# Hybrid decoder layer in float32: two plain weight loads moved ahead of the quarter B22 on SyncE's queue

## The chip, the cores and the metric

One core of one Trainium2 chip. The metric is device time in microseconds of one execution, as the median of three runs. Inputs and outputs are float32 in HBM; the weights (about 277 MB) are read once, in pieces of 512 KB.

## What is computed

One decoder layer for 256 tokens, D_MODEL 2048, D_FF 5632, 16 heads of 128. Cut to what matters:

```python
h = rmsnorm(x, g_mix)
proj = h @ w_in                                 # 2048 x (3*2048 + 3*2048): q, k, v and three gates
gates = sigmoid(proj[..., 3 * MIX_WIDTH:])
...                                             # three attention branches on q, k, v
merged = (gates[:, :, 0] * (flat(o_a) @ w_branch[:ea])
          + gates[:, :, 1] * (flat(o_b) @ w_branch[ea:eb])
          + gates[:, :, 2] * (flat(o_c) @ w_branch[eb:]))
x = x + merged @ w_out
h2 = rmsnorm(x, g_ffn)
gu = h2 @ w_gu                                  # 2048 x (2*5632)
x = x + (silu(gu[..., :D_FF]) * gu[..., D_FF:]) @ w_down
```

## The kernel before, in words

**Numbers in two halves.** Every float32 operand is split into a high part, rounded to the type that TensorE multiplies at full rate, and a low part, the rest. `split` (L108) does it with a cast on ScalarE (`w_hi`) and a subtraction on VectorE (`w_lo`). `product` (L161) then makes one product of three matmuls, hi*hi (L163), hi*lo (L164) and lo*hi (L165); each has 128 rows of weights and streams 512 columns into one PSUM bank.

**Stages.** First q, k, v and the gates (`w_in`), with attention work fed in between; then the branch projections (`w_branch`), the output projection (`w_out`), the FFN's first product (`w_gu`) and its second (`w_down`).

**Pairs.** q with k (4 times), two gate columns (5 times) and the FFN's gate and up columns (11 times) are computed by `project_pair` (L324): two columns of 512, A and B, against the 256 tokens at once. Of the 2048 rows of the weights, the first 1024 (two chunks of 512, `WC`) go through a scheme of seven products in place of eight: the weights of a chunk are four quarters B11, B12, B21 and B22 (first or second half of its rows, column A or B), and the seven forms multiply sums of the quarters with sums of the activations that are kept ready. The other 1024 rows are plain: four loads per column, which the prediction calls k0 to k3 for column B. One pair holds 180 matmuls of 512 columns.

The four PSUM banks of a pair are X, Y, Z and V (named `ps`/`qs` and, from the second gates pair on, `z`/`v` in the profile). The order of the program is: form 1 (B11) into X, snapshot of X; form 2 (B21) into Y; form 5 (u, the sum of B11 and B12) into Z, snapshot of Z; then the loads of B22; then plain k0 and k1 into V and Z; u += B22 and form 6 (u) into X, snapshot; plain k2; B12 += B22 and form 7 into X, snapshot; plain k3; form 3 (B22) into Z; and then column A: plain k0, k1, u += B21, form 4, plain k2, k3. A snapshot (L304) is a copy by ScalarE; the bank goes on being added to, so TensorE cannot write it again before the copy has read it. At its end a pair calls `begin_pair` (L314) for the next: this loads B11, B12 and B21 and splits B11 and B21.

**Loads.** `load` (L281) issues one DMA of 512 KB on SyncE's queue. Quarters go into `g_raw`, six buffers, two for each quarter (one per chunk); plain loads go into `w_raw`, four buffers. With six buffers for eight quarter loads per pair, the loads of B22 take the buffers of B11 of the same pair, and the plain loads k0 and k1 take the buffers of k0 and k1 of column A of the pair before. `fetch` (L104) pins these DMAs in the order of the program, and an instruction that waits on SyncE's queue holds all behind it. `parts` (L287) makes `w_hi` and `w_lo` of a load; there are five buffers of each, and every call also moves other work on by a step (`stages`).

**Order elsewhere.** The kernel runs under a scheduler that places the instructions of TensorE, VectorE and ScalarE by its own estimate of when their inputs are ready; only pinned ones keep the program's order. After a pair its results are taken over in the next one: for gates by `keep_gate` (L668), four sigmoid activations (L671) on ScalarE whose results GpSimd's queue writes out (L672); for the FFN two activations (L861) and two products (L862).

Of the kernel before, what the change touches and what calls it, by code (L numbers as in the profile page):

```python
# [56 lines left out]
def hybrid_block(ctx: ExitStack, tc: tile.TileContext, x, w_in, w_branch, w_out, w_gu, w_down, rel_bias, xT, gains,  # L57
# [24 lines left out]
    def pool(stack, name, side, bufs=1):  # L82
        return stack.enter_context(tc.tile_pool(name=name, bufs=bufs, side=side, reuse_waits="tile"))
# [8 lines left out]
    def half_kb(dt=F32):  # L92

        return scratch.tile([P, NB], dt, name="sc")
# [3 lines left out]
    def banks():  # L98

        turn.reverse()  # L100
        return [acc.tile([P, NB], F32, name=turn[1]) for _ in range(2)]
# [6 lines left out]
    def split(hi, lo, src, pin=False):  # L108
        for op in nc.scalar.copy(hi, src), nc.vector.tensor_sub(lo, src, hi.bitcast(F32)):  # L109
            if pin:  # L110
                tc.keep_in_program_order(op)
# [19 lines left out]
    def advance(queue):  # L131
        while queue:
            try:
                next(queue[0])
                return
            except StopIteration:
                queue.pop(0)
# [23 lines left out]
    def product(ps, ah, al, wh, wl, start=False, stop=False):  # L161
        how = dict(skip_group_check=True)
        nc.tensor.matmul(ps, ah, wh, start=start, stop=False, **how)  # L163
        nc.tensor.matmul(ps, ah, wl, start=False, stop=False, **how)  # L164
        nc.tensor.matmul(ps, al, wh, start=False, stop=stop, **how)  # L165
# [115 lines left out]
    def load(w, k, col0, pl=None):  # L281

        raw = pl.tile([P, 2, NB], F32, name="g_raw", bufs=6 if pl is gx else 4) if pl else wpool.tile([P, 2, NB], F32, name="w_raw", bufs=4)
        (nc.sync.dma_start if w is w_down else fetch)(raw, w[k * P:(k + 2) * P, col0:col0 + NB].rearrange("(k p) n -> p k n", p=P))
        return raw

    def parts(src):  # L287
        hi = wpool.tile([P, 2, NB], F32R, name="w_hi")
        lo = wpool.tile([P, 2, NB], F32R, name="w_lo")
        split(hi, lo, src)  # L290
        advance(stages)
        split_count[0] += 1
        if split_count[0] % 2:
            advance(slow_stages)
        for step in at_split.pop(split_count[0], ()):
            step()
        return hi, lo
# [4 lines left out]
    def snapshot(ps):  # L302
        sb = half_kb()
        nc.scalar.copy(sb, ps)  # L304
        return sb

    def add_into(dsts, srcs):
        for d, a in zip(dsts, srcs):
            tc.keep_in_program_order(nc.vector.tensor_add(d, d, a))  # L309

    def quarter(acts, w, kh, col0):
        return [load(w, 4 * c + 2 * kh, col0, gx) for c in acts.wc]

    def begin_pair(acts, w, colA, colB):  # L314

        b11, b12 = (quarter(acts, w, 0, col0) for col0 in (colA, colB))
        p11 = [parts(b) for b in b11]
        u = [gx.tile([P, 2, NB], F32, name="u") for _ in acts.wc]
        for a, b, d in zip(b11, b12, u):
            nc.vector.tensor_add(d, a, b)  # L320
        b21 = quarter(acts, w, 1, colA)
        return p11, b12, u, b21, [parts(b) for b in b21]

    def project_pair(acts, w, colA, colB, begun=None, nxt=None):  # L324

        cols = (colA, colB)
        X, Y = banks()
        Z, V = others()  # L330

        def form(ps, f, srcs, start, stop, split=False):
            for i, c in enumerate(acts.wc):
                wh, wl = srcs[i] if split else parts(srcs[i])
                for j in range(2):
                    product(ps, *acts.form(f, c, j), wh[:, j], wl[:, j], start and i + j == 0,
                            stop and i + j == len(acts.wc))

        def rest(n, k, p0, p1, start=False, stop=False):
            wh, wl = parts(load(w, k, cols[n]))  # L340
            for t, ps in ((1, p1), (0, p0)):
                for j in range(2):
                    product(ps, *acts.plain(t, k + j), wh[:, j], wl[:, j], bool(start and t == 1 and j == 0), stop and j == 1)

        ks = [k for c in range(KT // 4) if c not in acts.wc for k in (4 * c, 4 * c + 2)]
        p11, b12, u, b21, p21 = begun or begin_pair(acts, w, colA, colB)
        form(X, 1, p11, True, True, True)
        s1 = snapshot(X)
        form(Y, 2, p21, True, False, True)
        form(Z, 5, u, True, True)  # L350
        z5 = snapshot(Z)
        b22 = quarter(acts, w, 1, colB)
        rest(1, ks[0], Z, V, start=True)
        rest(1, ks[1], Z, V)
        add_into(u, b22)
        form(X, 6, u, False, True)
        x2 = snapshot(X)
        rest(1, ks[2], Z, V)
        add_into(b12, b22)
        form(X, 7, b12, False, True)  # L360
        x3 = snapshot(X)
        rest(1, ks[3], Z, V, stop=True)
        nc.vector.tensor_sub(z5, z5, x3)
        c22 = half_kb()
        nc.vector.tensor_add(c22, V, z5)
        form(Z, 3, b22, False, True)
        c12 = half_kb()
        nc.vector.tensor_sub(c12, Z, x2)
        for k in ks[:2]:
            rest(0, k, Y, X)  # L370
        add_into(u, b21)
        form(X, 4, u, False, False)
        for k in ks[2:]:
            rest(0, k, Y, X, stop=k == ks[-1])
        ahead = begin_pair(*nxt) if nxt else None
        c11 = half_kb()
        nc.vector.tensor_add(c11, Y, s1)
        return (c11, X, c12, c22), ahead
# [9 lines left out]
    p1 = pool(ph1, "p1", "left")  # L388
# [343 lines left out]
    for (kind, what), after in zip(units, units[1:] + [(None, None)]):  # L732
        if kind == "gates" and what[0] == chunks[4]:
            finish_stages(slow_stages)
            pat.close()
            acc2 = ctx.enter_context(tc.tile_pool(name="acc2", bufs=1, space=PSUM))
            others = beside
            o = Columns(pool(ph1, "o", "left"), "o", NH)
            for i in range(NH // 4):
                at_split[split_count[0] + 22 * i + 14] = [lambda k=4 * i: split_o(k)]  # L740
        nxt = pair_of(*after)
        if kind in ("qk", "gates"):
            ps, ahead = project_pair(*pair_of(kind, what), ahead, nxt)
            if others is in_turn:
                turn.reverse()
        else:
            ps = project(h, 0, w_in, 0, KT, V0 + what * NB if kind == "v" else gate_col(*what),
                         *((ps0, FIRST) if (kind, what) == ("v", 0) else ()))
            ahead = begin_pair(*nxt) if nxt else None
        finish_stages(stages)  # L750
        if kind == "v":
            keep_v(what, ps)
        elif kind == "qk":
            keep_qk(what, *ps)
        elif kind == "gate":
            keep_gate(*what, ps)
        else:
            keep_gate(*what[0], ps[:2])
            keep_gate(*what[1], ps[2:])
# [96 lines left out]
    for c in range(D_FF // NB):  # L856
        nxt = (h2, w_gu, (c + 1) * NB, D_FF + (c + 1) * NB) if c + 1 < D_FF // NB else None
        (g0, g1_, u0, u1), ahead = project_pair(h2, w_gu, c * NB, D_FF + c * NB, ahead, nxt)
        sg = [half_kb() for _ in range(NT)]
        for t, (g, u) in enumerate(((g0, u0), (g1_, u1))):  # L860
            nc.scalar.activation(sg[t], g, AF.Silu, scale=rstd2[:, t:t + 1])  # L861
            nc.vector.scalar_tensor_tensor(sg[t], u, rstd2[:, t:t + 1], sg[t], op0=ALU.mult, op1=ALU.mult)  # L862
        stages.append(to_a(c, sg))
# [153 lines left out]
```

## Time and profile before

| what | value |
| --- | --- |
| median of 3 runs | 1430.11 us (1429.63 to 1432.79) |
| the profiled execution, its own time | 1431.52 us |
| its span, first to last instruction | 1429.8 us |
| granted TensorE clock, mean | 1.00 |
| busy: TensorE, VectorE, ScalarE, GpSimd | 99%, 83%, 62%, 5% |
| HBM read, mean rate | 293.17 MB, 215 GB/s over the span |
| the last three gates pairs (w_in) | about 424 to 545 us |
| FFN pairs (w_gu) | about 730 to 1190 us |

In rows of single instructions the first number is the start in us from the span's start, the second the duration in us, then engine, line, operation, and output <- inputs by the program's names. PE is TensorE, ACT ScalarE, DVE VectorE, SPq SyncE's queue; a number in brackets is the idle time of the engine ahead of the instruction and what ended it. Rows that begin with one engine's name and an arrow say for whom it waited, in us: in total, how often, the longest. Rows that begin with a stretch (A:B) give its length, then TensorE's busy time and instructions in it, the granted clock, and the DMA share and rate. The end of a matmul is modelled, so starts are more reliable than ends.

### The profile page before, as it was taken

To read this page: it belongs to the slowest core of one execution; us is meant where nothing else is said; L and a number is where in the kernel's file an instruction comes from. 1 tells how busy PE (TensorE), PEld (TensorE's weight loads), DVE (VectorE), ACT (ScalarE), POOL (GpSimd) and SP (SyncE) were. 2 spreads that over 40 slices of the span, in tenths; PEclk is the share of its full clock that TensorE was granted. 3 is DMA by queue.
4 is the path that set the end of the run, shared out by engine and by line. 5 is a ranking of instruction groups with operands and counts; after the bars stand their busy time and mean duration, and the time that the engine had idled before them with its cause. 6 is when DMAs were issued, how large, how long until landed. Compare 5 with 4: busy or idle time off the path is not lost.

```text
span 1429.8 us, 17687 instructions
## 1 busy us (share of the span) xinstructions
PE 1416.7 (99%) x6369; PEld 1167.6 (82%) x6369; DVE 1192.8 (83%) x1265; ACT 881.4 (62%) x1136; POOL 65.2 (5%) x121
## 2 busy tenths in 40 slices
PE   9999999999999999999999999999999999999998
PEld 6888788888887778888888888888888888788887
DVE  7898797857798886876689999999999998886775
ACT  7777777667666665444457666666666666554453
POOL 1000000000000002100100000000000010100000
PEclk9999999999999999999999999999999999999999
DMA  9864547374656757876786556666665666767552
GB/s 327 279 221 134 206 137 245 112 247 157 222 188 223 254 195 268 297 229 213 222 299 221 198 182 218 224 226 227 220 210 192 231 212 230 251 235 235 190 172 95
DMA packets 155048, 309.05 MB, mean 216 GB/s; under 512 B 10792, under 2 KB 13376, under 8 KB 154960
## 3 DMA queue, kind: packets, MB, share of 16 engines
q1 hardware_dynamic: 144672, 277.38, 57.7%
q0 software_dynamic: 8992, 29.45, 6.1%
q10 hardware_dynamic: 1296, 1.08, 0.2%
q8 instruction: 50, 0.82, 0.2%
q14 instruction: 38, 0.31, 0.1%
HBM read 293.17 MB, written 14.70 MB: 215 GB/s over the span
## 4 chain that ended last, share of the span: by engine, by line
PE 81%; DVE 8%; DMA 4%; issue 3%; ACT 2%; SPq 0%; DVEq 0%; ACTq 0%
PE ps L164 9%; PE qs L164 9%; PE qs L165 9%; PE ps L165 9%; PE ps L163 9%; PE qs L163 9%; DVE w_lo L109 4%; PE z L163 4%; PE z L164 4%; PE z L165 4%; PE v L164 2%; PE v L165 2%; PE v L163 2%; DMA w_raw<-in_w_in 2%; PE tr L185 1%
## 5 line engine op out<-in xcount | busy, mean ns | idle before, releaser
L109 DVE TENSOR_TENSOR w_lo<-w_raw,w_hi 128x1024 fp32r<-128x1024 f32 x332 | 403.1, 1221 | 110.9 <-ACT w_hi L109 107.5
L109 ACT CAST w_hi<-w_raw 128x1024 fp32r<-128x1024 f32 x332 | 346.4, 1051 | 167.4 <-PE qs L165 59.9
L109 ACT CAST w_hi<-g_raw 128x1024 fp32r<-128x1024 f32 x184 | 192.2, 1053 | 146.9 <-PE ps L165 42.9
L109 DVE TENSOR_TENSOR w_lo<-g_raw,w_hi 128x1024 fp32r<-128x1024 f32 x184 | 219.6, 1221 | 35.1 <-ACT w_hi L109 33.8
L109 ACT CAST w_hi<-u 128x1024 fp32r<-128x1024 f32 x138 | 144.9, 1053 | 141.4 <-DVE u L309 71.3
L109 DVE TENSOR_TENSOR w_lo<-u,w_hi 128x1024 fp32r<-128x1024 f32 x138 | 165.7, 1220 | 24.9 <-ACT w_hi L109 24.0
L164 PE MATMUL ps<-w_lo,h_hi 128*128 128x512 f32 x352 | 137.9, 392 | 1.5 <-DVE w_lo L109 1.5
L165 PE MATMUL ps<-w_hi,h_lo 128*128 128x512 f32 x352 | 137.3, 390 | 0.0
L163 PE MATMUL ps<-w_hi,h_hi 128*128 128x512 f32 x352 | 132.4, 391 | 0.0
L164 PE MATMUL qs<-w_lo,h_hi 128*128 128x512 f32 x332 | 129.7, 391 | 0.0
L165 PE MATMUL qs<-w_hi,h_lo 128*128 128x512 f32 x332 | 129.2, 390 | 0.0
L163 PE MATMUL qs<-w_hi,h_hi 128*128 128x512 f32 x332 | 123.6, 391 | 0.0
L309 DVE TENSOR_TENSOR u<-u,g_raw 128x1024 f32<-128x1024 f32 x80 | 94.6, 1218 | 0.0
L164 PEld LDWEIGHTS ps<-w_lo,h_hi 128*128 128x128 f32 x352 | 66.1, 188 | 15.9 <-DVE w_lo L109 2.3
L165 PEld LDWEIGHTS ps<-w_hi,h_lo 128*128 128x128 f32 x352 | 66.1, 188 | 13.6
L163 PEld LDWEIGHTS ps<-w_hi,h_hi 128*128 128x128 f32 x352 | 65.9, 188 | 13.4
L165 PEld LDWEIGHTS qs<-w_hi,h_lo 128*128 128x128 f32 x332 | 62.4, 188 | 12.9
L164 PEld LDWEIGHTS qs<-w_lo,h_hi 128*128 128x128 f32 x332 | 62.4, 188 | 12.7
L163 PEld LDWEIGHTS qs<-w_hi,h_hi 128*128 128x128 f32 x332 | 62.3, 188 | 12.7
L320 DVE TENSOR_TENSOR u<-g_raw 128x1024 f32<-128x1024 f32 x40 | 48.6, 1218 | 22.7 <-DMA g_raw<-in_w_in 18.4
L164 PE MATMUL v<-w_lo,h_hi 128*128 128x512 f32 x120 | 47.4, 395 | 1.8 <-DVE w_lo L109 1.8
L163 PE MATMUL v<-w_hi,h_hi 128*128 128x512 f32 x120 | 47.7, 397 | 0.1
(383 smaller groups left out, 2925.8 us busy)
## 6 DMA issues: line engine op xcount, KB each, us to landing
w_raw<-in_w_in SPq DMA_DIRECT2D x116, 512.0 KB, 4.8
g_raw<-in_w_gu SPq DMA_DIRECT2D x88, 512.0 KB, 5.1
w_raw<-in_w_gu SPq DMA_DIRECT2D x88, 512.0 KB, 6.2
g_raw<-in_w_in SPq DMA_DIRECT2D x72, 512.0 KB, 5.9
w_raw<-in_w_down SPq DMA_DIRECT2D x64, 512.0 KB, 4.6
w_raw<-in_w_branch SPq DMA_DIRECT2D x32, 512.0 KB, 5.9
w_raw<-in_w_out SPq DMA_DIRECT2D x32, 512.0 KB, 4.8
g_raw<-in_w_down SPq DMA_DIRECT2D x24, 512.0 KB, 5.1
```

The source lines that it names most:

```text
L109: for op in nc.scalar.copy(hi, src), nc.vector.tensor_sub(lo, src, hi.bitcast(F32)):
L163: nc.tensor.matmul(ps, ah, wh, start=start, stop=False, **how)
L164: nc.tensor.matmul(ps, ah, wl, start=False, stop=False, **how)
L165: nc.tensor.matmul(ps, al, wh, start=False, stop=stop, **how)
L185: nc.tensor.transpose(pt[:, i, :], src[:, i * P:(i + 1) * P], ident)
L309: tc.keep_in_program_order(nc.vector.tensor_add(d, d, a))
L320: nc.vector.tensor_add(d, a, b)
```

## The change

In `project_pair`, the plain loads k0 and k1 of column B are issued ahead of the two loads of B22 and handed to `rest`, which loads by itself only when it is given nothing:

```diff
-        def rest(n, k, p0, p1, start=False, stop=False):
-            wh, wl = parts(load(w, k, cols[n]))
+        def rest(n, k, p0, p1, start=False, stop=False, raw=None):
+            wh, wl = parts(raw or load(w, k, cols[n]))
...
         z5 = snapshot(Z)
+        first = [load(w, k, cols[1]) for k in ks[:2]]
         b22 = quarter(acts, w, 1, colB)
-        rest(1, ks[0], Z, V, start=True)
-        rest(1, ks[1], Z, V)
+        rest(1, ks[0], Z, V, start=True, raw=first[0])
+        rest(1, ks[1], Z, V, raw=first[1])
         add_into(u, b22)
```

So the order on SyncE's queue, per pair, goes from six quarter loads, two of B22, k0, k1, k2, k3 to six quarter loads, k0, k1, two of B22, k2, k3. The number of loads, their sizes and the buffers stay. The scheduler, which sees the new order, also places some instructions anew:

- TensorE: in the third to fifth gates pair and the second FFN pair the first matmul of k0 into V stands ahead of the last eleven of form 5 into Z, instead of behind them; in some of the first FFN pairs a few more matmuls and transposes change places.
- ScalarE: in the same four pairs the cast of k0 stands ahead of the activations that take over the pair before. In the first FFN pair one cast of form 7 goes ahead of the snapshot of X; in the fifth the snapshot of Z goes ahead of both casts of form 6, and an activation pair (L861) between the casts of form 5.
- VectorE: nothing moves in the qk and gates pairs; in the first, second, fourth and fifth FFN pairs a few subtractions and small products change places.
- GpSimd: nothing moves.

## The prediction, made before the changed kernel had run

> **What bounds the kernel now.** I read the page first, then the busy time by windows, then the single matmuls around each place where TensorE stops.
>
> ```profile
> span 1429.8 us, 17687 instructions
> PE 1416.7 (99%) x6369; PEld 1167.6 (82%) x6369; DVE 1192.8 (83%) x1265; ACT 881.4 (62%) x1136; POOL 65.2 (5%) x121
> ...
> 939.23:1190.00 250.77, 250.77 (x1131) 1.00 0.65 220
> ```
>
> TensorE is the bound: 99% of the span, and in the six FFN pairs from 939 to 1190 us it never stops. So the order of loads can only win back moments in which PE stood still. Busy time hides these in part, because each matmul's end is modelled. The starts show them:
>
> ```profile
> 466.97 0.39 PE L164 MATMUL qs<-w_lo,h_hi 128*128 128x512 f32 x1
> ...
> 469.24 0.39 PE L165 MATMUL qs<-w_hi,h_lo 128*128 128x512 f32 x1
> ...
> 474.45 0.39 PE L165 MATMUL z<-w_hi,b_slo 128*128 128x512 f32 x1
> 474.98 0.49 PE L163 MATMUL v<-w_hi,h_hi 128*128 128x512 f32 x1
> 476.24 0.50 PE L164 MATMUL v<-w_lo,h_hi 128*128 128x512 f32 x1 [0.77 <-DVE w_lo L109]
> 476.57 0.39 PE L165 MATMUL v<-w_hi,h_lo 128*128 128x512 f32 x1
> ```
>
> The first two are ten starts apart, so a 512-column matmul costs 2.27 / 10 = 0.227 us. From 474.45 to 476.57 three starts take 2.12 us in place of 0.68: this place cost 1.44 us. Two waits (0.53 - 0.227 and 1.26 - 0.227) make 1.33 of it; the 0.11 left over is a slow start after the wait (0.33 in place of 0.227). The matmuls that waited are the first of the plain load k0, into V. Who was late is read in the other engines:
>
> ```profile
> 447.82 8.50 SPq L106 DMA_DIRECT2D g_raw<-in_w_in  x6
> ...
> 465.09 1.50 SPq L106 DMA_DIRECT2D g_raw<-in_w_in  x2
> 466.65 17.04 SPq L106 DMA_DIRECT2D w_raw<-in_w_in  x7
> ...
> SPq L106 <- DVE w_lo L109: 25.2, 8, 8.7
> ...
> 466.65 7.15 DMA w_raw<-in_w_in
> ...
> 473.87 1.05 ACT L109 CAST w_hi<-w_raw 128x1024 fp32r<-128x1024 f32 x1 [1.62 <-DMA w_raw<-in_w_in]
> 475.18 1.05 ACT L109 CAST w_hi<-w_raw 128x1024 fp32r<-128x1024 f32 x1 [0.26 <-DMA w_raw<-in_w_in]
> ...
> 474.95 2.53 DVE L109 TENSOR_TENSOR w_lo<-w_raw,w_hi 128x1024 fp32r<-128x1024 f32 x2 [3.62 <-ACT w_hi L109]
> 477.40 2.35 DVE L309 TENSOR_TENSOR u<-u,g_raw 128x1024 f32<-128x1024 f32 x2
> ```
>
> SyncE issued b11, b12 and b21 by 456.32, then stood until 465.09: b22 needs the buffers of b11, and its queue's longest wait is 8.7 us, for the w_lo that reads them. Only then came k0, at 466.65, and it landed 7.15 us later. ScalarE sat idle 1.62 us for it, VectorE 3.62 us, and PE stopped. The chain is b22's buffer, k0's issue, k0's landing, cast, subtraction, matmul.
>
> **The change part by part.** It adds and removes no instruction and no byte. In each of the 20 pairs (4 qk, 5 gates, 11 FFN) two 512 KB loads pass the two of b22 on SyncE's queue; no other queue's order moves, GpSimd's included. What else moves is the scheduler's work, which I take from the built order.
>
> *The loads.* k0 and k1 now wait only for the w_raw buffers of the pair before:
>
> ```profile
> 451.30 1.22 DVE L109 TENSOR_TENSOR w_lo<-w_raw,w_hi 128x1024 fp32r<-128x1024 f32 x1
> ...
> DMA to landing us min/median/max: 3.5/6.1/12.3
> ...
> DMA to landing us min/median/max: 3.5/4.9/6.6
> ```
>
> The second of these is read out at 452.52, before b21's last issue ends at 456.32. So this wait is over when SyncE comes to it, and b22, which is queued behind it, is not held. k0 leaves at about 456.4. The first landing row is that of all w_raw loads from 400 to 560 us: 3.5 to 12.3 us puts k0 between 459.9 and 468.7, against 473.8. I take the median 6.1, 462.5. b22 still leaves at 465.09 and 466.22. By the second row (g_raw, same stretch) it lands by 472.8 at the latest; its first reader, the add at 477.40, will come at 475.8 (below). Both ends cost nothing, since the first cast of k0 cannot start before 469.67 anyway.
>
> *The casts, three gates pairs from 424 us on and the second FFN pair.* The built order puts k0's cast ahead of the L671 activations (L861 in the FFN).
>
> ```profile
> 467.17 2.19 ACT L109 CAST w_hi<-u 128x1024 fp32r<-128x1024 f32 x2 [1.89 <-PE ps L165]
> 471.69 0.56 ACT L304 COPY sc<-qs 128x512 f32<-128x512 f32 x1
> ...
> 476.13 0.58 ACT L304 COPY sc<-z 128x512 f32<-128x512 f32 x1
> ```
>
> w_hi has five buffers, so k0's cast needs the matmuls of b11's second half, whose last starts at 469.24 and ends 0.39 later, and 0.03 from one engine to the next (the cast ends at 474.92, its subtraction starts at 474.95): 469.67. It ends at 470.7. The activations and the first snapshot, which now fill the time from u's casts (469.36) to 472.25, 2.9 us, follow and end at 473.6. k1's cast ends at 474.6, the subtraction behind it at 475.8, b22's adds (2.35 us) at 478.1, where before they ended at 479.75. PE comes to k0's second matmul at 474.9 and finds its w_lo, which half of the 2.53 us after 470.7 makes ready at 472.0. Then the copy of Z: it waits for Z's last matmul (474.68 now) and ends near 475.7; PE writes Z again at 476.0. That is the tightest place, 0.3 us.
>
> *The matmuls.* In the same four pairs the first V matmul of k0 moves ahead of the last eleven of Z, to about 472.19 (474.45 less ten steps). Its cast has ended 1.4 us earlier. The matmul at 474.98 did not let later ones pass while it waited. The Trainium skill ("TensorE: Matmul & The Clock Gate", "Step-by-step: what each phase is for") says the same as a rule: matmuls stay in program order and only weight loads are pulled ahead. By that rule a late k0 would now hold eleven matmuls of Z too and the sum would turn (third rival); by the rows k0 is early and the sum stays.
>
> **The sum.** Places that hang on this chain, each as its excess over 0.227 plus 0.11:
>
> ```profile
> 432.73 0.39 PE L163 MATMUL v<-w_hi,h_hi 128*128 128x512 f32 x1
> 433.57 0.50 PE L164 MATMUL v<-w_lo,h_hi 128*128 128x512 f32 x1 [0.45 <-DVE w_lo L109]
> ...
> 444.39 0.39 PE L163 MATMUL ps<-w_hi,b_shi 128*128 128x512 f32 x1
> 444.86 0.50 PE L164 MATMUL ps<-w_lo,b_shi 128*128 128x512 f32 x1
> ...
> 516.95 0.39 PE L163 MATMUL v<-w_hi,h_hi 128*128 128x512 f32 x1
> 517.96 0.50 PE L164 MATMUL v<-w_lo,h_hi 128*128 128x512 f32 x1 [0.62 <-DVE w_lo L109]
> ...
> 528.78 0.39 PE L163 MATMUL ps<-w_hi,b_shi 128*128 128x512 f32 x1
> 529.26 0.50 PE L164 MATMUL ps<-w_lo,b_shi 128*128 128x512 f32 x1
> ...
> 751.98 0.39 PE L163 MATMUL qs<-w_hi,h_shi 128*128 128x512 f32 x1
> 752.76 0.50 PE L164 MATMUL qs<-w_lo,h_shi 128*128 128x512 f32 x1 [0.40 <-DVE w_lo L109]
> ...
> 911.39 0.39 PE L163 MATMUL qs<-w_hi,h_shi 128*128 128x512 f32 x1
> 911.86 0.50 PE L163 MATMUL z<-w_hi,h_hi 128*128 128x512 f32 x1
> ```
>
> Gates: 0.72 (432.73) + 0.35 (444.39) + 1.44 (474.45) + 0.89 (516.95) + 0.36 (528.78) = 3.76. The two on b_shi are the later forms of the same pairs; I read them as the same lateness handed on by VectorE, whose adds of b22 (477.40) stand behind k0's subtraction, so I count them whole.
>
> FFN, fifth pair, 911.39: PE waits for ScalarE's copy of Z, which stands behind casts that ran late, and the built order moves it ahead of both casts of u: 0.35.
>
> ```profile
> 906.25 1.06 ACT L109 CAST w_hi<-w_raw 128x1024 fp32r<-128x1024 f32 x1 [0.25 <-DMA w_raw<-in_w_gu]
> 911.22 0.59 ACT L304 COPY sc<-z 128x512 f32<-128x512 f32 x1
> ...
> 748.70 2.35 DVE L309 TENSOR_TENSOR g_raw<-g_raw 128x1024 f32<-128x1024 f32 x2
> 749.91 0.59 ACT L304 COPY sc<-qs 128x512 f32<-128x512 f32 x1 [3.10 <-PE qs L165]
> ```
>
> FFN, first pair, 751.98: the cast that PE wants stood behind the copy at 749.91, though its add was done at about 749.9. The built order lets one cast go first: it ends at 751.0, its w_lo at 752.25, and PE needs it at 752.2. Of 0.66 I count 0.5; none to all is possible.
>
> Sum: 3.76 + 0.35 + 0.5 = 4.6 us. The other pairs have no PE stop that hangs on a load, and everything behind a removed stop moves forward as a whole. The profiled execution took 1431.52 us (its span and 1.7 around it), 0.1% over the median of the three runs, 1430.11. It would take 1426.9; on the median's scale that is **1425.5 us**, 0.3% less.
>
> **The rivals.**
>
> *Something else is late next.* The 0.3 us ahead of the copy of Z is the thinnest margin. If the activations make ScalarE 0.8 us later than worked out, each of the four pairs with the new cast order pays 0.5: 4.6 - 2.0 = 2.6, 1427.5 us. Against it: ScalarE is 62% busy over the span, and k0's cast comes 4.2 us earlier (473.87 to 469.67). Chance 0.18.
>
> *Nothing gained: VectorE was the cause.* It is 83% busy over the span. If its own work sets the end of a pair, the stops only move: within 1 us of 1430.1. Against it: the 3.62 us in which it sat idle ahead of k0. Chance 0.13.
>
> *Slower: k0 blocks the queues in front of which it was put.* Place: the hoisted V matmul at 472.19, and ScalarE's queue, where the four activations, the snapshots and all later casts stand behind k0's cast. It costs nothing as long as k0 lands by 472.19 - 1.05 - 0.1 = 471.0, 14.6 us after its issue. Were it to land as before, at 473.8, the cast would end at 474.9 and each of the four pairs would pay 2.9 us, 11.6 in all against the 4.1 that these four lose now: 1437.6 us. Equal is reached at a landing of about 471.9, 15.5 us after the issue; the longest in the row is 12.3. Chance 0.06.
>
> That the change does not do what it says is excluded by the built order of SyncE's queue.
>
> **How the numbers follow.** Forecast 0.63 (1424 to 1427), the rivals 0.18, 0.13 and 0.06. About 0.2%, 2.9 us, is what a measurement can tell from no change, so faster means under 1427.2: the forecast and two thirds of the first rival, 0.75; same 0.19; slower 0.06. The range goes from 1423.5 (all of the 0.66, and the 0.5 by which the fastest run lies under the median) to 1429.6, which takes in the first rival and half of the second.
>
> **What would show it.** Right: on SyncE two w_raw issues stand between b21 and b22, about 9 us earlier in the pair; the starts v L163 to v L164 in the gates pairs are 0.227 apart; ScalarE no longer waits for w_raw<-in_w_in there. The first pair of the FFN shows alone whether the 0.5 was right. Wrong: a wait of PE for a copy of Z (first rival), the same length of a gates pair with PE waiting for w_lo of u (second), or a stop at the hoisted V matmul with Z's matmuls behind it (third).

## The result, and the profile after

The changed kernel takes 1427.54 us (median of 11 runs, 1426.06 to 1429.03), the kernel before, on the same chip, 1430.57 us (11 runs, 1429.0 to 1432.9). The ratio is 0.9975, 95% interval 0.9966 to 0.9985: 3.0 us faster, where 4.6 us were forecast. Two more sets of runs of the same changed kernel gave 0.9973 (0.9963 to 0.9983) and 0.9967 (0.9955 to 0.998). The profiled execution took 1428.19 us itself. Its page:

```profile
span 1426.5 us, 17719 instructions
PE 1415.7 (99%) x6369; PEld 1168.7 (82%) x6369; DVE 1191.6 (84%) x1265; ACT 880.0 (62%) x1136; POOL 65.2 (5%) x121
```

Nothing is to be seen there: TensorE was 99% busy and still is. The change shows only where it works. These are the rows of the fourth of the five gates pairs in the changed kernel, the one whose stop at 474.45 us opens the prediction: SyncE's queue, ScalarE, VectorE, TensorE (lines below 351 have moved by one, so the activation is L672).

```profile
455.37 0.37 SPq L106 DMA_DIRECT2D g_raw<-in_w_in  x1
455.83 0.93 SPq L106 DMA_DIRECT2D w_raw<-in_w_in  x2
464.51 1.50 SPq L106 DMA_DIRECT2D g_raw<-in_w_in  x2
...
469.50 1.06 ACT L109 CAST w_hi<-w_raw 128x1024 fp32r<-128x1024 f32 x1 [0.30 <-PE qs L165]
470.46 0.72 ACT L672 ACTIVATE sc<-sc,rstd 128x512 f32<-128x512 f32 x1
...
474.94 0.59 ACT L304 COPY sc<-z 128x512 f32<-128x512 f32 x1 [0.55 <-PE z L165]
...
470.67 1.23 DVE L109 TENSOR_TENSOR w_lo<-w_raw,w_hi 128x1024 fp32r<-128x1024 f32 x1
474.43 1.23 DVE L109 TENSOR_TENSOR w_lo<-w_raw,w_hi 128x1024 fp32r<-128x1024 f32 x1 [2.53 <-ACT w_hi L109]
...
472.02 0.39 PE L163 MATMUL v<-w_hi,h_hi 128*128 128x512 f32 x1
472.25 0.39 PE L164 MATMUL z<-w_lo,b_shi 128*128 128x512 f32 x1
...
474.52 0.39 PE L165 MATMUL z<-w_hi,b_slo 128*128 128x512 f32 x1
474.75 0.39 PE L164 MATMUL v<-w_lo,h_hi 128*128 128x512 f32 x1
474.97 0.39 PE L165 MATMUL v<-w_hi,h_lo 128*128 128x512 f32 x1
```

k0 and k1 leave at 455.83, right behind b21. SyncE still stands before b22 (464.51), but nothing urgent is behind it now. The cast of k0 waits for a buffer that TensorE frees (0.30 us), no longer for the load, and TensorE's starts are 0.23 us apart from the first V matmul to the last row: the stop of 1.44 us is gone. How long the two loads took to land (min/median/max):

```profile
L106 SPq DMA_DIRECT2D w_raw<-in_w_in x2: 420/420/420, 455.8 to 456.3; - x2
...
DMA to landing us min/median/max: 6.5/6.9/7.3
```

So they land between 462.3 and 463.6, and k0's cast starts at 469.50: some 6 us to spare. A transfer of 12.3 us, the longest of before, would still have landed at 468.1, ahead of the cast.

To see where the whole gain lies, I take the starts of the same two matmuls in two executions and subtract: the length of a stretch, free of what came ahead of it. The five stops of the sum lie in the last three gates pairs (432.73 and 444.39 in the third, 474.45 in the fourth, 516.95 and 528.78 in the fifth); the first two pairs take the same time, to 0.1 us, in all executions. For the stretch with the five stops the two matmuls are these, first in the kernel before, then in the changed one:

```profile
424.12 0.39 PE L165 MATMUL qs<-w_hi,h_lo 128*128 128x512 f32 x1
...
540.05 0.39 PE L163 MATMUL ps<-w_hi,h_hi 128*128 128x512 f32 x1
```

```profile
425.11 0.39 PE L165 MATMUL qs<-w_hi,h_lo 128*128 128x512 f32 x1
...
537.08 0.39 PE L163 MATMUL ps<-w_hi,h_hi 128*128 128x512 f32 x1
```

115.93 us became 111.97: 3.96 us less, against 3.76 in the sum. The same subtraction for the places that the argument needs, for all executions told of below, in us. Stretches are named by the clock of the first profile of before; "k0 early" says whether k0 of the gates pairs is issued without a wait of b22 ahead of it; the names are those of the experiments. Two places are left out, because they differ as much among kernels of either kind: the first 40 us (39.4 to 41.1) and the attention work from 160 to 180 us (19.3 to 22.0).

| execution | k0 early | q, k 235-260 | gates pairs 3 to 5, 424-540 | branch 573-586 | FFN 1st pair 745-762 | FFN 2nd 787-803 | FFN 5th 900-915 | down 1205-1270 |
| --- | --- | --- | --- | --- | --- | --- | --- | --- |
| before, first profile | no | 24.95 | 115.93 | 12.98 | 17.03 | 16.09 | 15.13 | 64.84 |
| e5_before_again | no | 25.04 | 113.88 | 13.33 | 17.03 | 16.53 | 15.43 | 63.47 |
| e10_before_three | no | 24.95 | 115.20 | 12.85 | 17.07 | 16.27 | 14.75 | 64.04 |
| e3_qk_only | no | 24.93 | 114.15 | 13.10 | 17.03 | 16.13 | 14.75 | 63.75 |
| e6_ffn_only | no | 24.94 | 115.15 | 13.33 | 16.32 | 16.82 | 14.75 | 63.55 |
| changed, first profile | yes | 26.24 | 111.97 | 12.49 | 16.32 | 16.78 | 14.75 | 65.61 |
| e1_again | yes | 25.33 | 111.97 | 12.82 | 16.32 | 16.78 | 14.75 | 63.47 |
| e9_again_two | yes | 26.49 | 111.97 | 12.49 | 16.32 | 16.78 | 14.75 | 63.78 |
| e2_gates_only | yes | 25.73 | 111.97 | 12.49 | 17.15 | 16.09 | 14.79 | 63.91 |
| e4_eight_buffers | yes | 24.95 | 111.97 | 12.49 | 17.16 | 16.09 | 15.49 | 65.63 |
| e8_k0_only | yes | 24.94 | 111.97 | 12.73 | 17.05 | 16.09 | 14.75 | 64.37 |
| e7_cast_first | yes | 24.92 | 111.97 | 12.91 | 16.32 | 16.09 | 14.75 | 64.42 |
| e11_cast_first_two | yes | 25.41 | 111.97 | 12.49 | 16.32 | 16.09 | 14.75 | 64.82 |

The first profile of after beside the first of before: gates -3.96, first FFN pair -0.71, fifth -0.38, branch -0.49, but q and k +1.29, second FFN pair +0.69, down stage +0.77. All that the sum names went; what was given back lies in three places that it doesn't name. The experiments ask which of these belong to the change.

### The profile page after: what moved, and what is told of

Read it like the earlier page. It is cut to its first block, busy times and chain, and to the rows that moved or that the text cites. A ratio compares the mean times of both kernels' runs of the same rounds, so it can differ in the third digit from the quotient of the medians.

```text
span 1426.5 us, 17719 instructions
## 1 busy us (share of the span) xinstructions
PE 1415.7 (99%) x6369; PEld 1168.7 (82%) x6369; DVE 1191.6 (84%) x1265; ACT 880.0 (62%) x1136; POOL 65.2 (5%) x121
## 4 chain that ended last, share of the span: by engine, by line
PE 89%; DVE 5%; DMA 2%; issue 2%; ACT 1%; SPq 0%; DVEq 0%; ACTq 0%
PE qs L164 10%; PE ps L164 10%; PE qs L165 10%; PE qs L163 10%; PE ps L165 10%; PE ps L163 10%; PE z L164 4%; PE z L165 4%; PE z L163 4%; PE v L164 3%; PE v L165 3%; PE v L163 3%; DVE w_lo L109 2%; PE tr L185 1%; PE tr L165 1%
## 5 line engine op out<-in xcount | busy, mean ns | idle before, releaser
L309 DVE TENSOR_TENSOR g_raw<-g_raw 128x1024 f32<-128x1024 f32 x40 | 47.1, 1221 | 0.0
```

## The experiments

The theory: b22's wait for the buffers of b11 holds k0 on SyncE's queue, k0 lands late, TensorE stops; an early k0 removes just that. The rivals: the stops are VectorE's and only move; or the moved loads themselves cause the 1.3 us lost in q and k and the 0.8 in the down stage.

**The changed kernel once more, nothing edited (e1_again).**

> The changed kernel once more, nothing altered, for a second profile of it. About 1427.5 us on the scale where the kernel before takes 1430.6. In the first profile all stops of the sum were gone, but three places were 2.6 us longer than before: 1.3 us near 246 to 250 us (q and k), 0.65 us near 790 us (second FFN pair), 0.67 us from 1221 to 1240 us (down stage). Theory: the stop near 790 us comes from the changed order on ScalarE, so it is here again, 0.6 to 0.7 us; the other two hang on when a transfer happens to land, so they are here smaller, larger or gone, by several tenths of a us each. Rival: all three are caused by the moved loads; then all three are here again within 0.2 us of their sizes.

Measured: 1426.4 us against 1430.2, ratio 0.9973. The second FFN pair has its 0.69 us again, the down stage (63.47) nothing at all, q and k 0.38 instead of 1.29. So the first is built in, and the others depend on the execution.

**The loads moved in the gates pairs alone (e2_gates_only), and in q and k alone (e3_qk_only).**

```diff
-        first = [load(w, k, cols[1]) for k in ks[:2]]
+        first = [load(w, k, cols[1]) for k in ks[:2]] if w is w_in and colA >= NH * HD else [None, None] 
+        first = [load(w, k, cols[1]) for k in ks[:2]] if w is w_in and colA < NH * HD else [None, None]    # e3
```

> The two loads are moved ahead of B22 in the five gates pairs alone; q, k and FFN pairs as before. Theory (b22's wait for the buffers of b11 holds the issue of k0): the five stops of the gates pairs, 3.76 us in the sum, are gone, so 1430.6 - 3.8 = 1426.8 us or, with the 0.5 us that the changed kernel also won in the branch stage behind them, down to 1426.3; the stop of the first FFN pair, 0.66 us near 752 us, is back. Rival (VectorE sets the end of a pair): 1430 to 1430.6, the stops only move.

> The two loads are moved in the four pairs of q and k alone. If the 1.3 us that the changed kernel lost near 246 to 250 us are caused by the moved loads: 1430.6 + 1.3 = 1431.9 us, with VectorE's sum of B11 and B12 waiting longer for the load of B12 than before. If they were the chance of one execution: 1430.6 us, within 0.4.

Measured: e2 1427.59 us against 1430.2, ratio 0.9979 (0.997 to 0.9988); e3 1429.97, ratio 0.9994 (0.9984 to 1.0005). The gates pairs alone bring 2.6 us where 3.8 were expected, and moving the loads of q and k costs nothing that can be measured. The loss in q and k can be watched: VectorE's sum of B11 and B12 waits for the load of B12 (the bracket), and 23 us later TensorE, in its attention work (L580), waits for VectorE. First the changed kernel, then e2, whose q and k pairs issue their loads as before, then e3, whose loads are moved there:

```profile
227.17 1.23 DVE L320 TENSOR_TENSOR u<-g_raw 128x1024 f32<-128x1024 f32 x1 [8.63 <-DMA g_raw<-in_w_in]
...
250.36 0.45 PE L580 MATMUL att<-kT,qT 128*128 128x256 f32 x1 [0.53 <-DVE p L588]
```

```profile
229.43 1.22 DVE L320 TENSOR_TENSOR u<-g_raw 128x1024 f32<-128x1024 f32 x1 [8.11 <-DMA g_raw<-in_w_in]
...
252.62 0.45 PE L580 MATMUL att<-kT,qT 128*128 128x256 f32 x1 [0.53 <-DVE p L588]
```

```profile
225.11 1.23 DVE L320 TENSOR_TENSOR u<-g_raw 128x1024 f32<-128x1024 f32 x1 [7.07 <-DMA g_raw<-in_w_in]
```

A wait over 8 us and its stop come without a moved load (e2); with one (e3) the wait is 7.07 us and no stop follows. The loss follows the wait for that landing: in the eight executions whose stretch takes 25.04 us or less the wait is 6.8 to 7.4 us; 7.72 and 7.79 us go with 25.33 and 25.41, and 8.11, 8.63 and 9.02 us with 25.73, 26.24 and 26.49. With moved loads the stretch averages 25.5 us over the seven such executions of the table, without 25.1 over six; whether the moved k0 makes the bad case more frequent, these few profiles can't say.

**No load moved, two more buffers (e4_eight_buffers).** `g_raw` has eight buffers in place of six during the first stage, so that b22 takes none of b11's.

```diff
-    WC = (0, 1)
+    WC, gbufs = (0, 1), [8]
-        raw = pl.tile([P, 2, NB], F32, name="g_raw", bufs=6 if pl is gx else 4) ...
+        raw = pl.tile([P, 2, NB], F32, name="g_raw", bufs=gbufs[0] if pl is gx else 4) ...
-    gx = pool(h2_stack, "gx2", "left", 2)
+    gx, gbufs[0] = pool(h2_stack, "gx2", "left", 2), 6
```

> No load is moved: the kernel before, with eight buffers for the quarters in place of six during the first stage (q, k, gates), so that b22 takes no buffer of b11. Theory (the wait for the buffer is what held k0, and the order of the queue matters only through it): the same as the run with the loads moved in the gates pairs alone, about 1426.8 us, SyncE's stand of 8.7 us ahead of b22 gone, and k0 landed before its cast can start at 469.7 us. Rival (k0 has to stand ahead of b22 in the queue, since the transfers of b22 and the two extra issues of 1.1 us each delay it): the stops stay, 1430 us or a little under.

Measured: 1426.03 us against 1430.2, ratio 0.9972 (0.996 to 0.9984). SyncE's queue and the two ends of the gates stretch:

```profile
446.28 8.50 SPq L106 DMA_DIRECT2D g_raw<-in_w_in  x8
454.88 16.46 SPq L106 DMA_DIRECT2D w_raw<-in_w_in  x5
...
424.15 0.39 PE L165 MATMUL qs<-w_hi,h_lo 128*128 128x512 f32 x1
...
536.12 0.39 PE L163 MATMUL ps<-w_hi,h_hi 128*128 128x512 f32 x1
```

All eight quarter loads leave without a stand, the plain loads follow at 454.88 in the old order, and the stretch is 111.97 us again, the changed kernel's to 0.01. This is the test of the cause: the order on the queue mattered through the buffer that b22 waits for. It fits what the Trainium skill ("Perfetto Trace Analysis", "DMA Instruction — HWDGE (DVE, Sync)") says, that the queue's sequencer itself sits out a DMA's semaphore wait and takes the next instruction after it; here that cost k0 the 8.7 us of b22.

One thing came along: in e2, e4 and e8, too, the scheduler put k0's cast ahead of the activations and moved the first V matmul forward, as in the changed kernel. Whether an early k0 needs that new order is answered further down, by e5.

**Half of the change: k0 alone moved (e8_k0_only).**

```diff
-        first = [load(w, k, cols[1]) for k in ks[:2]]
+        first = [load(w, ks[0], cols[1]), None]
```

> Half of the change: k0 alone is moved ahead of the two loads of B22, in all pairs; k1 stays behind them. Theory (only k0's landing decides): k1 now takes the place behind b22 that k0 had, lands about 473.8 us on the clock of the first profile, its low part is ready at about 476.1, and TensorE wants it at 477.6, so the gates pairs hold no more than 0.5 us and the time is 1430.9 - 2.8 = 1428 us or less. Rival (k1 is late next): a stop at k1's first low matmul, 1 us or more in each of the three later gates pairs, so that no gain is left: 1430 to 1431 us.

Measured: 1427.49 us against 1431.61, ratio 0.9969 (0.9958 to 0.9981); the gates stretch is 111.97 once more. The landing of one 512 KB load decided all five stops; k1 had slack where it stood.

**The kernel before, twice more (e5_before_again, e10_before_three).**

> The kernel before once more, for a second profile of its stops. In the first profile the gates pairs (424 to 540 us) held 3.96 us more than the same matmuls took in the three kernels whose k0 came early; in the run with the loads of q and k moved, whose gates pairs issue their loads as before, they held only 2.17. Theory: the stop is how much later than needed k0 lands, so its size changes from execution to execution; here between 1.5 and 4.5 us. Rival: 3.96 is the fixed price of the order of the loads, and the 2.17 came from the moved loads of q and k; then 3.96 within 0.3 here.

> The kernel before a third time, for one more sample of its stops. In the four executions so far whose gates pairs issue k0 behind b22 these pairs held 3.96, 2.17, 1.91 and 3.08 us, mean 2.8; here again something between 1.5 and 4.5. A value under 0.5 would speak against the theory that k0 behind b22 is late in every execution.

Measured: 1430.67 and 1429.62 us, one run each, and a gates stretch of 113.88 and 115.20. With e3, e6 and the first profile there are five executions whose k0 stands behind b22. In the order first profile, e5, e10, e3, e6 they hold 3.96, 1.91, 3.23, 2.18 and 3.18 us over 111.97, mean 2.9 (the 3.08 in the last expectation is e6's 3.18). So the stop isn't a fixed price. In the fourth pair it can be followed to the landing. The rows are from the chains of waits in e3, e5 and e6 (start of the issue, us to landing):

```profile
465.22 6.10 DMA w_raw<-in_w_in
```

```profile
466.95 7.25 DMA w_raw<-in_w_in
```

```profile
469.12 6.60 DMA w_raw<-in_w_in
```

With landings after 6.10, 6.33 (e10), 6.60, 7.15 (the first profile) and 7.25 us the fourth pair is 0.40, 0.73, 0.92, 1.47 and 1.34 us longer than in the changed kernel (stretch from 460 to 482 us): about a microsecond of landing, a microsecond of stop.

In the gates pairs these executions have the engines' old order. Over their third to fifth pairs, 15 in all, ScalarE's wait ahead of k0's cast runs from 0.05 to 1.62 us, and the stops from 0 to 1.47. The 0.05 is in e5's third pair, where k0 landed 5.97 us after its issue: ScalarE comes to the cast straight from the copy, TensorE's starts stay 0.23 us apart, and the stretch from 424 to 440 us is as long as in the changed kernel:

```profile
431.47 0.56 ACT L304 COPY sc<-ps 128x512 f32<-128x512 f32 x1
432.08 1.05 ACT L109 CAST w_hi<-w_raw 128x1024 fp32r<-128x1024 f32 x1
...
434.46 0.39 PE L163 MATMUL v<-w_hi,h_hi 128*128 128x512 f32 x1
434.69 0.39 PE L164 MATMUL v<-w_lo,h_hi 128*128 128x512 f32 x1
434.91 0.39 PE L165 MATMUL v<-w_hi,h_lo 128*128 128x512 f32 x1
```

So an early k0 is enough in the old order, too: the new place of the cast and of the V matmul isn't what removes the stop. (In its fifth pair e5 has 0.04 us at k0 and still 0.5 us near 529, at the later form on b_shi; what caused that was not followed.)

**The loads moved in the FFN pairs alone (e6_ffn_only).** The edit is that of e2 with the condition `w is w_gu`.

> The two loads are moved in the eleven FFN pairs alone; q, k and gates as before. Theory: the stop near 752 us in the first FFN pair goes (-0.69) and one of the same size comes in the second, near 795 us (+0.69), since there the cast now stands behind the copy on ScalarE; the fifth pair's stop hangs on a landing and is 0 to 0.4 us with or without the change. Sum 0: 1430.2 us, within 0.5, and the gates pairs keep their stops, 1.5 to 4.5 us. Rival (the prediction's sum): 0.35 + 0.5 less, 1429.3 us.

Measured: 1430.88 us against 1431.15, ratio 0.9999 (0.999 to 1.0008): nothing. The first pair's stop goes (17.03 to 16.32) and the second gets one (16.09 to 16.82). These rows of the changed kernel show why (ScalarE, VectorE, TensorE), and below them ScalarE in the kernel before at the same place:

```profile
787.92 0.59 ACT L304 COPY sc<-ps 128x512 f32<-128x512 f32 x1 [3.56 <-PE ps L165]
788.41 2.00 ACT L109 CAST w_hi<-g_raw 128x1024 fp32r<-128x1024 f32 x2
...
786.02 2.36 DVE L309 TENSOR_TENSOR g_raw<-g_raw 128x1024 f32<-128x1024 f32 x2
789.49 2.36 DVE L109 TENSOR_TENSOR w_lo<-g_raw,w_hi 128x1024 fp32r<-128x1024 f32 x2 [1.11 <-ACT w_hi L109]
...
789.99 0.39 PE L163 MATMUL ps<-w_hi,h_shi 128*128 128x512 f32 x1
790.77 0.50 PE L164 MATMUL ps<-w_lo,h_shi 128*128 128x512 f32 x1 [0.39 <-DVE w_lo L109]
```

```profile
791.92 1.06 ACT L109 CAST w_hi<-g_raw 128x1024 fp32r<-128x1024 f32 x1 [3.75 <-DVE g_raw L309]
792.88 0.58 ACT L304 COPY sc<-ps 128x512 f32<-128x512 f32 x1
```

The first add on `g_raw` is done at about 787.2 (half of the 2.36 us from 786.02), but ScalarE stands at the copy, which waits 3.56 us for TensorE's last matmul into X; the cast comes at 788.41, its subtraction at 789.49, and TensorE waits. Before, the cast went ahead of the copy. The second pair now has the fault that the first had before, a ready cast behind a waiting copy. The list in "The change" leaves this swap on ScalarE out. The Trainium skill ("Perfetto Trace Analysis", "Tensor Engine Instruction (MATMUL, LD_WEIGHTS)") calls ScalarE's queue strictly first in, first out; the 1.2 us in which a ready cast stood behind a waiting copy agree.

**The cast pinned ahead of the copy in the second FFN pair (e7_cast_first, and again e11_cast_first_two), beside the changed kernel a third time (e9_again_two).**

```diff
-        x2 = snapshot(X)
-        rest(1, ks[2], Z, V)
-        add_into(b12, b22)
-        form(X, 7, b12, False, True)
+        x2 = None if second else snapshot(X)       # second: w is w_gu and colA == NB
+        rest(1, ks[2], Z, V); add_into(b12, b22)
+        p12 = [parts(b12[0], True), x2 := snapshot(X, True), parts(b12[1], True)][::2] if second else b12
+        form(X, 7, p12, False, True, second)
```

(Shortened: `True` keeps the cast or the copy in program order, and the helpers `split`, `parts` and `snapshot` pass it on.)

> The changed kernel, with one cast of form 7 pinned ahead of the copy of X on ScalarE in the second FFN pair. Theory: the stop near 791 us (0.55 + 0.11, with its two neighbours 0.69 in all) is gone and nothing comes in its place: 0.7 us less than the changed kernel, 1426.3 us where that takes 1427.0. Rival: the cast's source is not ready earlier and it is VectorE that is late there; then the stop stays and the time is the changed kernel's, within 0.2.

> The changed kernel a third time, beside the run with the cast pinned. About 1427 us; all five stops of the gates pairs gone and a stop of 0.69 us near 790 us, as in both profiles so far. The stretches from 162 to 165 and 246 to 250 us and the down stage from 1210 to 1260 us differ between the profiles so far by up to 1.8, 1.3 and 2.3 us, in kernels with and without moved loads there; if that is the chance of the landings, they differ here again.

> The changed kernel with the cast pinned in the second FFN pair, once more. No stop near 752 and none near 791 us, gates pairs as in the changed kernel; 1426.3 us by the first time, or 0.7 under the changed kernel's 1426.4 to 1427.5, so 1425.7 to 1426.8.

Measured: e7 1426.28 us and e9 1426.75 (five runs each) against 1431.15, ratios 0.9966 (0.9953 to 0.9978) and 0.9967 (0.9955 to 0.998); e11 1426.97 us against 1431.61, 0.9969 (0.9958 to 0.9981). In e7 the row order is the one asked for and the stop is gone:

```profile
787.57 1.05 ACT L109 CAST w_hi<-g_raw 128x1024 fp32r<-128x1024 f32 x1 [2.99 <-DVE g_raw L309]
788.53 0.58 ACT L304 COPY sc<-ps 128x512 f32<-128x512 f32 x1
...
790.21 0.39 PE L163 MATMUL ps<-w_hi,h_shi 128*128 128x512 f32 x1
790.43 0.39 PE L164 MATMUL ps<-w_lo,h_shi 128*128 128x512 f32 x1
```

The second pair takes 16.09 us in both profiles, the first keeps its 16.32. So 0.69 us are won back in the trace. By the clock this version and the changed kernel cannot be told apart: 0.47 us where they ran side by side, and no difference in the ratios to before. It is the fastest version here by its stops, not by a measured median.

## Why the prediction was right, and where its size was off

**The cause: shown.** The stand before b22 made k0 late. Taking away b22's wait for a buffer (e4) or k0's place behind b22 (e2, e8) gives the same 111.97 us, and with k0 behind b22 the stop grows with the landing and is gone where the landing is early enough (e5's third pair).

**The loads, casts and matmuls: as worked out.** Issue 456.4 forecast, 455.83 measured; landing 462.5, measured 462.3 to 463.6 for the two; cast 469.67, measured 469.50; first V matmul 472.19, measured 472.02; k0's second matmul 474.9, measured 474.75, without a wait.

**The time alone would not have decided.** 1427.54 us lies a little outside the forecast's 1424 to 1427 and on the first rival's 1427.5; the other two sets of runs, 3.8 and 4.4 us faster, lie nearer the forecast's 4.6 than the rival's 2.6. The trace tells them apart: the rival's sign, TensorE waiting for a copy of Z, is nowhere in it. That the first set met the rival's time is chance: the forecast's stops went, but they were worth less on average, and a new one came.

**Gates, 3.76 us: right for that execution, too large for the median.** The profiled execution lost 3.96 us there, but five executions lose 2.9 on average. The step that failed is the last of the sum: "It would take 1426.9; on the median's scale that is 1425.5 us". The stops of one execution were taken off the median of others, although that execution was 1.4 us slower than the median, and 1.1 us of this was its longer stops. A stop that ends with a transfer's landing has a spread, and the sum needed its mean.

**FFN, first pair, 0.5 us: came, and went back.** It brought 0.71 us, and the second pair lost 0.69 against the first profile of before (16.09; 16.1 to 16.5 in the six executions with unmoved loads, 16.78 after). The step that failed is "The other pairs have no PE stop that hangs on a load, and everything behind a removed stop moves forward as a whole": the change also altered ScalarE's order in the second pair, where I looked only at k0's cast and not at the copy that went ahead of form 7's casts.

**FFN, fifth pair, 0.35 us: right size, but the reason wasn't needed.** I put it down to the built order of ScalarE. In e7, e8 and e11 the engines' order in the fifth pair is that of before and only its loads are moved, and it takes 14.75 us; with the loads unmoved it takes 14.75 to 15.49, by k0's landing: 14.75 after 6.35 and 6.38 us, 14.79 after 6.58, 15.13 after 7.06, 15.43 after 7.04 (issued 0.3 us later than the others) and 15.49 after 7.38. Moved, k0 is issued 10 us earlier. So the earlier load is enough, and before the change the stop was there in some executions only: over the six with unmoved loads 0.3 us on average. That 0.35 meets this mean is luck; one profile could as well have shown 0 or 0.74.

**The first rival (copy of Z), the second (VectorE), the third (queues blocked): none.** The copy waits for TensorE (474.94, 0.55 us) and not the other way round; it ends at 475.53, and TensorE writes Z again at 476.11, 0.58 us later where 0.3 were forecast. VectorE still waits 2.53 us for a cast, and no stop came back in any gates pair. The hoisted matmul found k0 long landed. (In the third rival's price, 4.1 should be 3.8: the fifth FFN pair's 0.35 is in it, but is not one of its four pairs. And the lower end of the range, 1423.5, does not follow from the two terms given for it: 1425.5 less 0.16 and 0.5 is 1424.8.)

**Added up:** 2.9 in the gates, 0.3 in the fifth FFN pair, 0 in the first two: 3.2 us, where the three sets measured 3.0, 3.8 and 4.4. The branch stage may belong to it: 12.6 us on average with k0 early, 13.1 without. No run isolates that, so it stays open. The losses of 1.29 and 0.77 us in the first profile of after are not shown to be a price of the change. The first follows a landing, late or not with and without moved loads. The down stage took 63.5 to 65.6 us in both kinds of kernel, and e4, which moves no load, was the longest; ScalarE's longest wait there for the FFN's products to be read back is 6.3 and 6.7 us in the two executions at 65.6 us and 3.3 and 4.1 in the two at 63.47, which points to a landing too, but no run tests it.

## What to carry to other kernels

A load that waits for its buffer holds every load behind it on that queue: look for the urgent one behind a waiting one, and either move it ahead or give the waiting one a buffer; both did the same here. When the price of a stop is read from one profile and the stop ends with a landing, take several profiles, or take its mean, before it is subtracted from a median. And where a scheduler builds the order, compare the whole built order in every repetition of the changed function, not only the instructions that were moved: here one swap on ScalarE gave back 0.69 us.

## What the hardware showed beside that

- With no load late, the gates stretch is the same to 0.01 us: 111.97 us in eight executions of five different kernels. With a late load it differs by up to 2 us between executions of one program (113.88 to 115.93).
- Standing ahead in the queue hardly made the transfer itself faster: in the fourth gates pair k0 took 5.7 to 6.7 us to land in the seven executions with it moved, and 6.1 to 7.3 us in the five with it behind b22. What helped was the issue some 11 us earlier.
